# Seven block products in place of eight in two feed-forward networks, with the hidden activations sent through DRAM

## The chip, the cores and the metric

The kernel runs on one core of one Trainium2 chip. Its time is the device time of one execution in microseconds, the median of several runs. Engines are named as in the profile: PE is TensorE (matmuls), PEld its weight loads, DVE is VectorE, ACT is ScalarE, POOL is GpSimd and SP is SyncE, which here issues every DMA.

## The reference

Two transformer layers, one after the other, on 1024 tokens of 1024 features in fp32. What the change touches are their two feed-forward networks, each with 2816 hidden features (22 tiles of 128):

```python
# layer 1
x = layer_norm(DEEPNORM_ALPHA * x + einsum('bse,ed->bsd', mix, w_out), ln1_g, ln1_b)
gate, up = (x @ w_gu)[..., :FFN_HIDDEN], (x @ w_gu)[..., FFN_HIDDEN:]
ffn = (silu(gate) * up) @ w_down
x = layer_norm(DEEPNORM_ALPHA * x + ffn, ln2_g, ln2_b)
...
# layer 2
x = x + gate_m * rmsnorm(mix, g_mix_post)
h = rmsnorm(x, g_ffn_pre) * (1.0 + scale_f) + shift_f
f = (silu(h @ w_gate) * (h @ w_up)) @ w_down
x = x + gate_f * rmsnorm(f, g_ffn_post)
```

The vectors `scale_f`, `shift_f` and four more come from one product of a condition vector with `w_cond`, which the kernel works out beside the first network.

## The kernel before

Every product of fp32 matrices is made of three matmuls: an operand is split into `hi` (a cast, on ACT, line 80) and `lo` (the rest, a subtraction, mostly on DVE, line 84), and hi·hi, hi·lo and lo·hi are added in PSUM. So each 128 x 128 block of weights times 512 tokens costs three matmuls of 128x512.

The activations stand feature-major, hi and lo, in tiles for each half of the tokens (`Act`). `Act.put` turns one token block of 128 by eight transposes on PE (line 766), casts on ACT (line 777) and subtracts on DVE (line 778). Blocks 0 to 3 are the first half, blocks 4 to 7 the second; in the trace the tiles are x10 and x11 for the first network and x30 and x31 for the second (with h or l for the part).

`ffn` runs over the 22 hidden tiles. For a tile and a half of the tokens `gate_up` makes 48 matmuls (eight feature tiles, gate and up, three each), then silu on ACT (line 835), the product (line 836) and the split of the result on DVE and ACT. The result stays in SBUF. After every two tiles `down` multiplies them with two row tiles of the down weights (lines 863 to 865), block after block of tokens, and DVE adds 128x512 pieces into the accumulators `acc` (line 720 in the first network, 1319 in the second). The last four tiles (three in the second network) end each token block with its residual and norm (`after`). The first two tiles take the first half of the tokens first: their 96 matmuls need nothing of the second half.

Layer 1's output projection and norm stand ahead of the first network (lines 693 to 695, 717, 720, 784 to 797), layer 2's ahead of the second (line 1179 to 1197). Beside the first network `cond(j)` works out the vectors of layer 2: six chunks of eight 512 KB loads and eight DVE steps (line 949), one after every third tile.

A scheduler orders the rows of each engine as the code is written; what stands under `soon()` is moved ahead. All engines run their rows in order. The loads of weights and those of layer 2's residuals go through one queue, SP.

Of the kernel before, what the change touches and what calls it, by code (L numbers as in the profile page):

```python
# [38 lines left out]
def two_blocks(ctx: ExitStack, tc: tile.TileContext, a):  # L39
# [55 lines left out]
    def mm3(out, lh, ll, rh, rl, start, stop):  # L95
        T.matmul(out, lh, rh, start=start, stop=False)  # L96
        T.matmul(out, lh, rl, start=False, stop=False)  # L97
        T.matmul(out, ll, rh, start=False, stop=stop)  # L98

    def rsqrt(v, n):  # L100
        """v: [P, n] -> 1/sqrt(v); v is overwritten"""
# [18 lines left out]
    # =====================================================================  # L120
    # block 1: input projection, indexer selection, attention, gMLP
    # =====================================================================
# [59 lines left out]
    # DRAM scratch  # L182
# [5 lines left out]
    # indexer keys (hi, lo, hi, lo over the partitions), indexer weights, values of C  # L188
# [17 lines left out]
    # the first token blocks follow the arrival of x  # L206
# [38 lines left out]
    class TopkSet:  # L245
# [39 lines left out]
        def settle(self):  # L285
            """a sign sum counts a tie by half: the result is the threshold or the number before it"""
# [17 lines left out]
        def mask(self):  # L304
            """scores -> additive mask with the distances; ties at the threshold go to the lowest keys"""
# [13 lines left out]
    def load_qk(pl, bufs, src, s):  # L319
        """[hi; hi], [lo; lo] of the queries and [hi; lo] of the keys of one head over 128 partitions"""  # L320
# [23 lines left out]
    def expo(qk, i, bias, slope):  # L344
        """exp(logits - max) and its sum; the products come divided by slope"""
# [30 lines left out]
    # pieces of the projections, to be put between the steps of other work  # L376
# [11 lines left out]
    def qk_pieces(u):  # L388
        """queries (scaled) and keys of a head of B or of two of C, hi and lo, to DRAM"""
# [123 lines left out]
    class Paced:  # L513
        """runs a generator at so many steps a turn"""
# [16 lines left out]
    # 1 - lam_init goes into the gain; neglam = -lam  # L531
# [14 lines left out]
    class LaneB:  # L546
        """a head of B after the other: weights() and then mix() of one token block after the other"""
# [52 lines left out]
    class LaneC:  # L600
        """the heads of C in pairs"""
# [71 lines left out]
    def turned(tb, c0):  # L673
        """columns c0 .. c0 + 512 of token block tb of the mixers' outputs, feature-major, hi and lo"""
# [11 lines left out]
    def out_block(wo, mt, tb, put):  # L686
        """half of the contraction of the output projection for token block tb"""
# [124 lines left out]
    def norm1(tb):  # L812
        layer_norm(acc[tb], g1, b1, G, V)
# [617 lines left out]
```

## Time and profile before

| what | value |
| --- | --- |
| median of three runs | 2656.75 us (2655.37 to 2658.04) |
| span of the profiled execution | 2659.7 us |
| PE busy | 2500.7 us, 94% |
| DVE busy | 1494.9 us, 56% |
| ACT busy | 916.3 us, 34% |
| POOL busy | 355.8 us, 13% |
| DMA | 262.91 MB, 99 GB/s on average |

The profiled execution's span lies 2.95 us above the median of the runs. The network of layer 1 runs from about 660 to 1425 us, that of layer 2 from about 1890 to the end. Matmuls overlap one another, so a PE at 100.00 us in 100 us says that it never stopped, not that no matmul could be packed closer.

### The profile page before, as it was taken

How to read it: one execution, taken by the hardware profiler on the slowest of the kernel's cores; microseconds unless marked ns; L12 is line 12 of the kernel's file. 1: busy time of each engine (PE TensorE's matmuls, PEld its weight loads, DVE VectorE, ACT ScalarE, POOL GpSimd, SP SyncE). 2: the span in 40 equal slices, each digit the busy share in tenths (PEclk: the TensorE clock that was granted, in tenths of full speed). 3: DMA queues.
4: the chain of work that ended last, by engine and by line, in shares of the span. 5: the costliest groups of instructions: out<-in, count | busy, mean ns of one | idle time of the engine just before them, and what ended most of it. 6: DMA issues, size and time to landing. Idle time of an engine off the chain costs nothing. (4 is left out here: it accounts for less than half of the span.)

```text
span 2659.7 us, 32099 instructions
## 1 busy us (share of the span) xinstructions
PE 2500.7 (94%) x12232; PEld 2068.2 (78%) x12232; DVE 1494.9 (56%) x2974; ACT 916.3 (34%) x1603; POOL 355.8 (13%) x250
## 2 busy tenths in 40 slices
PE   8889897899999999999999988898899999999997
PEld 8878776787778878878887777786688888888885
DVE  3889869648544444444367366768923333333337
ACT  4558774343211111111145235455731111111111
POOL 2220233112000000000020044327200000000002
PEclk9999998999999999999999999899999999999999
DMA  5154455422433232332223534643511111111112
GB/s 180 56 150 116 114 160 169 112 78 65 135 95 104 97 101 86 100 115 87 64 88 123 158 91 136 187 130 101 173 50 46 48 48 48 48 48 48 48 48 103
DMA packets 129333, 262.91 MB, mean 99 GB/s; under 512 B 17302, under 2 KB 63382, under 8 KB 129180
## 3 DMA queue, kind: packets, MB, share of 16 engines
q1 hardware_dynamic: 129180, 260.87, 31.7%
q8 instruction: 96, 1.57, 0.2%
q14 instruction: 57, 0.47, 0.1%
HBM read 206.27 MB, written 54.55 MB: 98 GB/s over the span
## 5 line engine op out<-in xcount | busy, mean ns | idle before, releaser
L80 ACT CAST wh<-raw 128x1024 fp32r<-128x1024 f32 x132 | 138.3, 1049 | 467.7 <-PE plg L97 381.7
L1319 DVE TENSOR_TENSOR acc<-acc,pmm 128x512 f32<-128x512 f32 x160 | 109.6, 686 | 233.9 <-PE pmm L865 232.9
L863 PE MATMUL pmm<-wdh,hh 128*128 128x512 f32 x576 | 227.9, 396 | 6.9 <-DVE acc L1319 3.8
L84 DVE TENSOR_TENSOR wl<-raw,wh 128x1024 fp32r<-128x1024 f32 x107 | 130.8, 1223 | 176.9 <-ACT wh L80 144.4
L865 PE MATMUL pmm<-wdh,hl 128*128 128x512 f32 x576 | 226.4, 393 | 0.0
L864 PE MATMUL pmm<-wdl,hh 128*128 128x512 f32 x576 | 226.4, 393 | 0.0
L720 DVE TENSOR_TENSOR acc<-acc,pmm 128x512 f32<-128x512 f32 x160 | 109.0, 684 | 147.1 <-PE pmm L865 140.8
L835 ACT ACTIVATE silu<-plg 128x512 f32<-128x512 f32 x88 | 52.2, 594 | 350.4 <-PE plg L98 350.3
L338 PE MATMUL plg<-qk,qk 128*128 128x384 f32 (+4 forms) x480 | 125.2, 376 | 21.1 <-DVE mn L351 6.7
L96 PE MATMUL plg<-x10h,wh 128*128 128x512 f32 x352 | 139.6, 397 | 4.9 <-ACT wh L80 4.9
L96 PE MATMUL plg<-x30h,wh 128*128 128x512 f32 x352 | 140.3, 400 | 1.4 <-ACT x30h L777 1.4
L97 PE MATMUL plg<-x30l,wh 128*128 128x512 f32 x352 | 140.4, 399 | 0.7 <-DVE x30l L778 0.7
L98 PE MATMUL plg<-x30h,wl 128*128 128x512 f32 x352 | 140.0, 398 | 0.0
L98 PE MATMUL plg<-x10h,wl 128*128 128x512 f32 x352 | 139.4, 396 | 0.1
L97 PE MATMUL plg<-x31l,wh 128*128 128x512 f32 x352 | 139.5, 396 | 0.0
L98 PE MATMUL plg<-x31h,wl 128*128 128x512 f32 x352 | 139.5, 396 | 0.0
L96 PE MATMUL plg<-x11h,wh 128*128 128x512 f32 x352 | 139.4, 396 | 0.0
L97 PE MATMUL plg<-x10l,wh 128*128 128x512 f32 x352 | 139.4, 396 | 0.0
L96 PE MATMUL plg<-x31h,wh 128*128 128x512 f32 x352 | 139.2, 396 | 0.0
L98 PE MATMUL plg<-x11h,wl 128*128 128x512 f32 x352 | 139.0, 395 | 0.0
L97 PE MATMUL plg<-x11l,wh 128*128 128x512 f32 x352 | 139.0, 395 | 0.0
L863 PEld LDWEIGHTS pmm<-wdh,hh 128*128 128x128 f32 x576 | 108.6, 189 | 36.5 <-DVE acc L1319 8.2
(351 smaller groups left out, 6306.4 us busy)
## 6 DMA issues: line engine op xcount, KB each, us to landing
raw<-in_wgu_dram SPq DMA_DIRECT2D x50, 512.0 KB, 3.6
raw_c<-in_w_cond_dram SPq DMA_DIRECT2D x48, 512.0 KB, 3.9
raw<-in_w_down_dram SPq DMA_DIRECT2D x44, 512.0 KB, 3.5
qk<-qkd SPq DMA_DIRECT2D x72, 256.0 KB, 6.5
qk<-qk2d SPq DMA_DIRECT2D x48, 256.0 KB, 4.8
raw<-in_wg_dram SPq DMA_DIRECT2D x22, 512.0 KB, 3.5
raw<-in_wu2f_dram SPq DMA_DIRECT2D x22, 512.0 KB, 4.0
raw<-in_wqk_dram SPq DMA_DIRECT2D x20, 512.0 KB, 3.7
```

The costliest lines, as they stand in the source:

```text
L80: A.copy(hi, src)
L84: eng.tensor_tensor(lo, src, hi.bitcast(F32), op=OP.subtract)
L96: T.matmul(out, lh, rh, start=start, stop=False)
L97: T.matmul(out, lh, rl, start=False, stop=False)
L98: T.matmul(out, ll, rh, start=False, stop=stop)
L338: T.matmul(pl[:, c, :n], q[:, isl], k2[:, c * n:(c + 1) * n], start=(j == 0), stop=last)
L720: V.tensor_tensor(acc[tb][:, dsl], acc[tb][:, dsl], o, op=OP.add)
L835: A.activation(s, pg[:, 0, :], AF.Silu)
L863: T.matmul(o, hh[:, ts], wh[:, dsl], start=(j == 0), stop=False)
L864: T.matmul(o, hh[:, ts], wl[:, dsl], start=False, stop=False)
L865: T.matmul(o, hl[:, ts], wh[:, dsl], start=False, stop=(j == n - 1))
L1319: V.tensor_tensor(acc2[tb][:, dsl], acc2[tb][:, dsl], o, op=OP.add)
```

## The change

Both networks are computed with Strassen's scheme (in Winograd's form): a matrix product of halves is made of seven block products and sums of blocks, where the plain way takes eight. All names below are those of the changed kernel.

For gate and up, `SAct` keeps the activations as quarters B11, B21, B22 (features by tokens) and the sums T1, T2, T3, T4, each in hi and lo parts. `put` of blocks 0 to 3 writes B11 and B21; `put` of blocks 4 to 7 writes B22, T3, T1 and T2, which need both halves of the tokens; `finish` makes T4 when all blocks are there. `Matrix` holds two hidden tiles of gate or of up, makes the weights' sums S1 to S4 on DVE, splits each operand, and runs seven products of 12 matmuls; `after` adds the products up. Eleven pairs of tiles take 11 x 2 x 7 x 12 = 1848 matmuls. The result goes to DRAM (`h_d`, line 992).

`down` then loads hidden tiles and down weights back (line 1065), 18 tiles in groups of 2 x (1, 2, 2, 2, 2), again as seven products each, with their sums and splits on DVE and POOL; the seven accumulators are combined in the last group. `down_last` does the last four tiles the plain way, and ends each token block. Layer 1's normed output goes to DRAM too (`x1_d`) and is added in `residual1`. `cond` runs after the pairs 1 to 6 of the first network.

The core of the diff:

```diff
+        def put(self, x, tb, affine=None):
...
+            t1, t2, t3 = self.temp(), self.temp(), self.temp()
+            V.tensor_tensor(t1, b12, b11[0], op=OP.subtract)
+            A.copy(t3, b22)
+            G.tensor_tensor(t1, t1, b11[1], op=OP.subtract)
+            V.tensor_tensor(t3, t3, b12, op=OP.subtract)
+            self.part("B22", ts, b22, V)
+            V.tensor_tensor(t2, b22, t1, op=OP.subtract)
+            self.part("T3", ts, t3, V)
+            self.part("T1", ts, t1, G)
+            self.part("T2", ts, t2, V)
+
+        def finish(self):
+            (bh, bl), (th, tl) = ([t.bitcast(F32) for t in self(n)] for n in ("B21", "T2"))
+            for c in range(4):
+                ts = slice(c * P, (c + 1) * P)
+                t = self.temp()
+                G.tensor_tensor(t, bh[:, :, ts], th[:, :, ts], op=OP.subtract)
+                G.tensor_tensor(t, t, bl[:, :, ts], op=OP.add)
+                G.tensor_tensor(t, t, tl[:, :, ts], op=OP.subtract)
+                self.part("T4", ts, t, G if c % 2 else V)
...
+        LEFT = {1: "A11", 6: "S2", 2: "A12", 7: "S3", 5: "S1", 4: "A22", 3: "S4"}
+        RIGHT = {1: "B11", 6: "T2", 2: "B21", 7: "T3", 5: "T1", 4: "T4", 3: "B22"}
...
+        def product(self, p):
...
+                A.copy(wh, x)
+                (G if p in (2, 4) else V).tensor_tensor(wl, x, wh.bitcast(F32), op=OP.subtract)
+            xh, xl = self.act(self.RIGHT[p])
+            first = p in (1, 6, 7, 5)
+            for k in range(4):
+                mm3(o, wh[:, k, :], wl[:, k, :], xh[:, k, :], xl[:, k, :], first and k == 0, k == 3, not first)
+            with soon():
+                self.after(p, o)
...
+            DMA.dma_start(h_d[self.f + i][:, l * 512:(l + 1) * 512], s)
...
+            if p == 0:
+                order = ((0, 1), (1, 1), (0, 2), (1, 2), *((m, q) for m in range(2) for q in (6, 7, 5, 4, 3)))
+            else:
+                order = tuple((m, q) for m in range(2) for q in (1, 6, 2, 7, 5, 4, 3))
...
+        def combine(p, c0, n):
+
+            x = {q: acc_of(q, c0, n) for q in range(1, 8)}
+            if p == 2:
+                G.tensor_tensor(x[2], x[2], x[1], op=OP.add)
+            elif p == 6:
+                G.tensor_tensor(x[6], x[6], x[1], op=OP.add)
+            elif p == 7:
+                G.tensor_tensor(x[7], x[7], x[6], op=OP.add)
+            elif p == 4:
+                G.tensor_tensor(x[4], x[7], x[4], op=OP.subtract)
+            elif p == 5:
+                V.tensor_tensor(x[6], x[6], x[5], op=OP.add)
+                G.tensor_tensor(x[7], x[7], x[5], op=OP.add)
+            elif p == 3:
+                V.tensor_tensor(x[3], x[6], x[3], op=OP.add)
...
+        for g, np_ in enumerate(sizes):
+            hr = [load2([h_d[f + np_ * i + j][:, :] for j in range(np_)], "hr") for i in range(2)]
+            wr = [load2([wd(f + np_ * i + j) for j in range(np_)], "wr") for i in range(2)]
...
+                        "S1": ("A21", "A22", OP.add, V), "S2": ("S1", "A11", OP.subtract, V),
+                        "S3": ("A11", "A21", OP.subtract, G), "S4": ("A12", "S2", OP.subtract, G),
+                        "T1": ("B12", "B11", OP.subtract, G), "T2": ("B22", "T1", OP.subtract, V),
+                        "T3": ("B22", "B12", OP.subtract, G), "T4": ("T2", "B21", OP.subtract, V)}[n]
...
+                    split(*hl, x, lo_eng="pool" if p in (1, 2, 4) else "dve")
+                    split(*wl, z, lo_eng="pool" if p in (1, 3) else "dve")
...
+                        if g == 0:
+                            A.copy(x, o)
+                        else:
+                            V.tensor_tensor(x, x, o, op=OP.add)
+                    if g == len(sizes) - 1:
+                        combine(p, c0, n)
...
+                split(*t, r, lo_eng="pool" if to is hs else "dve")
...
-    def extra1(ft):
-        if ft % 3 == 1 and ft // 3 < 6:
-            cond(ft // 3)
+    def extra1(p):
+        if 1 <= p <= 6:
+            cond(p - 1)
...
+    SIZES, NLAST = (1, 2, 2, 2, 2), 4
+    gate_up(x1, lambda f: a["wgu"][f], lambda f: a["wgu"][NFT + f], 5, 8, extra1)
...
+    y1 = down(dp, lambda f: a["w_down"][f], SIZES)
...
+    down_last(tp, lambda f: a["w_down"][f], NLAST, y1, residual1, after1, lambda: put_half(0))
```

Where rows stand on the engines, at three places.

On PE at the start of the second network the kernel before has the first tile's matmuls on the first half of the tokens (x30) right behind the output projection and a transposed block (L766); further blocks are transposed between them, and x31 comes after 96 of them and more:

```order
L695 MATMUL pmm<-woh_15234,mixl 128x512
L766 MATMUL ptr<-ident,acc 128x128 x8
L96 MATMUL plg<-x30h,wh 128x512 x2
L97 MATMUL plg<-x30l,wh 128x512
L98 MATMUL plg<-x30h,wl 128x512
```

In the changed kernel the same place reads as follows; x3B21 belongs to the first half of the tokens and is the last of the 48 matmuls of products 1 and 2, x3T2 is the operand of product 6:

```order
L98 MATMUL pmm<-x3B21l,wst 128x512
L99 MATMUL pmm<-x3B21h,wst 128x512
L815 MATMUL ptr<-ident,acc 128x128 x24
L97 MATMUL ptr<-x3T2h,wst 128x512
L98 MATMUL ptr<-x3T2l,wst 128x512
L99 MATMUL ptr<-x3T2h,wst 128x512
```

The transposes of the last three token blocks moved behind all matmuls on the first half, and the next matmul reads a sum to which every block of the second half contributes.

On DVE at the start of the first network, in the changed kernel, these rows follow the last token block (x1T2l is the last part of T2, x1T4l the parts of T4 whose input POOL makes, L922 the sums of weights and L943 the lo part of a weight operand, the first being that of product 6):

```order
L805 TENSOR_TENSOR x1T2l<-tt,x1T2h 128x4x128
L805 TENSOR_TENSOR x1T4l<-tt,x1T4h 128x4x128
L922 TENSOR_TENSOR tt<-rw 128x512
L805 TENSOR_TENSOR x1T4l<-tt,x1T4h 128x4x128
L922 TENSOR_TENSOR tt<-tt,rw 128x512
L922 TENSOR_TENSOR tt<-rw 128x512
L943 TENSOR_TENSOR wst<-tt,wst 128x512
```

The operand S2 of product 6 (the second L922 row) stands behind both parts of T4, which product 4 reads later on.

On SP between gate/up and down of the second network (the first network has the same rows), and on POOL at the end of the last down group (L84 lo parts, L1051 to L1058 combinations, `last` the hidden tiles of the plain end):

```order
L992 DMA h_d_6888<-p_19636 128x512
L992 DMA h_d_6887<-u_19658 128x512
L1065 DMA hr<-h_d_6867 128x1024
L1065 DMA hr<-h_d_6868 128x1024
L1065 DMA wr<-in_w_down_dram 128x1024 x2
```

```order
L84 TENSOR_TENSOR ws<-wr,ws 128x1024
L1055 TENSOR_TENSOR acc<-acc 128x512 x2
L1055 TENSOR_TENSOR acc<-acc 128x2x512
L1058 TENSOR_TENSOR acc<-acc,dacc_10151 128x512 x2
L1058 TENSOR_TENSOR acc<-acc,dacc_10151 128x2x512
L84 TENSOR_TENSOR last<-raw,last 128x1024 x4
```

In both, what the next stage needs first stands behind the last row of the stage before; before the change neither of these rows existed, since the hidden tiles never left SBUF.

## Rows read from the trace of the kernel before

**Rows 1.** The page: span, instructions, busy time of each engine.

```profile
span 2659.7 us, 32099 instructions
PE 2500.7 (94%) x12232; PEld 2068.2 (78%) x12232; DVE 1494.9 (56%) x2974; ACT 916.3 (34%) x1603; POOL 355.8 (13%) x250
```

**Rows 2.** Windows inside each network: length, busy us by engine (instructions), PEclk, DMA share, GB/s.

```profile
1000.00:1100.00 100.00, 100.00 (x432) 80.84 (x431) 46.77 (x57) 17.31 (x22) 0.00 (x0) 1.00 0.31 95
2200.00:2300.00 100.00, 100.00 (x431) 80.86 (x430) 33.25 (x43) 15.29 (x20) 0.00 (x0) 1.00 0.16 53
```

**Rows 3.** Waits of PE from 690 to 1400 us: total, times, longest.

```profile
PE pmm L863 <- DVE acc L720: 1.6, 3, 0.8
```

**Rows 4.** Windows at the networks' starts and ends, columns as in rows 2.

```profile
640.00:660.00 20.00, 19.62 (x92) 15.43 (x93) 19.36 (x46) 9.54 (x12) 4.80 (x2) 1.00 0.28 86
660.00:680.00 20.00, 13.65 (x61) 10.46 (x60) 19.42 (x30) 9.85 (x13) 5.55 (x2) 0.83 0.51 160
...
1400.00:1420.00 20.00, 16.17 (x75) 12.95 (x74) 18.62 (x61) 9.92 (x20) 4.80 (x2) 0.90 0.14 54
1860.00:1880.00 20.00, 17.48 (x81) 13.70 (x80) 19.76 (x57) 14.22 (x26) 7.68 (x4) 1.00 0.72 236
1880.00:1900.00 20.00, 13.98 (x57) 10.27 (x56) 19.86 (x59) 14.89 (x26) 3.09 (x1) 0.83 0.72 240
1900.00:1920.00 20.00, 20.00 (x96) 16.32 (x95) 17.52 (x60) 15.80 (x30) 4.80 (x2) 1.00 0.34 122
...
2609.00:2646.00 37.00, 31.67 (x125) 23.86 (x124) 33.46 (x75) 8.06 (x14) 15.55 (x7) 0.95 0.36 127
```

**Rows 5.** Groups by line and shape, 700 to 1450 us: busy, mean ns.

```profile
L720 DVE TENSOR_TENSOR acc<-acc,pmm 128x512 f32<-128x512 f32 x144 | 98.1, 684 | 141.3 <-PE pmm L865 140.8
L84 DVE TENSOR_TENSOR wl<-raw,wh 128x1024 fp32r<-128x1024 f32 x51 | 62.3, 1222 | 54.7 <-ACT wh L80 54.4
L949 DVE SCALAR_TENSOR_TENSOR mod<-raw_c,sc,mod 128x1024 f32<-128x1024 f32 x35 | 45.0, 1285 | 53.8 <-DMA raw_c<-in_w_cond_dram 53.8
L796 POOL TENSOR_TENSOR acc<-acc,g 128x1024 f32<-128x1024 f32 x6 | 14.5, 2422 | 709.7 <-ACT acc L795 703.7 <-PE pmm L865 6.0
```

**Rows 6.** Timeline of DVE, three neighbours: start, length.

```profile
1886.33 1.21 DVE L84 TENSOR_TENSOR wl<-raw,wh 128x1024 fp32r<-128x1024 f32 x1
1887.46 0.68 DVE L1179 TENSOR_TENSOR acc<-acc,pmm 128x512 f32<-128x512 f32 x1
1888.06 1.22 DVE L84 TENSOR_TENSOR wl<-raw,wh 128x1024 fp32r<-128x1024 f32 x1
```

**Rows 7.** Timeline: last put of layer 1's norm, PE around it.

```profile
674.03 0.79 PE L96 MATMUL plg<-x10h,wh 128*128 128x512 f32 x1 [4.92 <-ACT wh L80]
676.78 0.80 PE L96 MATMUL plg<-x11h,wh 128*128 128x512 f32 x1
...
678.76 1.27 DVE L778 TENSOR_TENSOR x11l<-ptr,x11h 128x512 fp32r<-128x512 f32 x2
```

**Rows 8.** Timeline: POOL and DVE side by side, 1799 to 1849 us.

```profile
1799.98 9.13 POOL L84 TENSOR_TENSOR wol<-raw,woh 128x1024 fp32r<-128x1024 f32 x3 [2.85 <-ACT woh L80]
1807.48 2.71 DVE L1227 TENSOR_TENSOR sab<-sab 128x1023 f32<-128x1023 f32 x1
...
1830.82 4.51 POOL L1174 TENSOR_TENSOR mixrow<-mixrow 128x512 f32<-128x512 f32 x2 [2.13 <-DMA mixrow<-mixT_d]
1834.67 0.68 DVE L1179 TENSOR_TENSOR acc<-acc,pmm 128x512 f32<-128x512 f32 x1
1848.68 2.56 POOL L1174 TENSOR_TENSOR mixrow<-mixrow 128x512 f32<-128x512 f32 x2 [1.97 <-DMA mixrow<-mixT_d]
```

**Rows 9.** Timeline: PE at the second network's start; last put.

```profile
1892.13 1.22 PE L96 MATMUL plg<-x30h,wh 128*128 128x512 f32 x2 [1.45 <-ACT x30h L777]
...
1934.43 0.69 DVE L778 TENSOR_TENSOR x31l<-ptr,x31h 128x512 fp32r<-128x512 f32 x1
```

**Rows 10.** DMA issues: KB each, median us from issue to landing.

```profile
raw<-in_w_down_dram SPq DMA_DIRECT2D x44, 512.0 KB, 3.5
```

More of the change, by code (lines that the diff above doesn't have):

```diff
@@ L93, in load_split, with mm3 @@
         return h, l
[L95 to L98, printed above, removed]
+    def mm3(out, lh, ll, rh, rl, start, stop, more=False):
+        T.matmul(out, lh, rh, start=start, stop=False, skip_group_check=more)
+        T.matmul(out, lh, rl, start=False, stop=False, skip_group_check=more)
+        T.matmul(out, ll, rh, start=False, stop=stop, skip_group_check=more)
     def rsqrt(v, n):
@@ L737, in two_blocks @@
     p1_done.close()
-    actp, act_done = pool("actp")
+    x1p, x1_done = pool("x1p")
     class Act:
@@ L809, in two_blocks @@
     b1 = row(slot("w", [P, D], F32, "ln1b"), a["ln1_b"])
-    x1 = Act(actp, "x1")
+    x1 = SAct(x1p, "x1")
+    x1_d = dr.tile([S, D], F32, name="x1_d")
     def norm1(tb):
         layer_norm(acc[tb], g1, b1, G, V)
+        DMA.dma_start(x1_d[tb * P:(tb + 1) * P, :], acc[tb])
     out_proj(wo, lambda tb: turned(tb, 512), add1, norm1, lambda tb: x1.put(acc[tb], tb), 2)
+    x1.finish()
     wo_done.close()
@@ new lines, in two_blocks, with out @@
+    class Gate(Matrix):
+        def out(self, i, l, t, o):
+            if t is None:
+                t = self.post("s11")
+                A.activation(t, o, AF.Silu)
+            else:
+                A.activation(t, t, AF.Silu)
+            self.p[i, l] = t
+    class Up(Matrix):
+        def out(self, i, l, t, o):
+            s = self.gate.p[i, l]
+            if t is None:
+                V.tensor_tensor(s, s, o, op=OP.mult)
+            else:
+                G.tensor_tensor(s, s, t, op=OP.mult)
+            DMA.dma_start(h_d[self.f + i][:, l * 512:(l + 1) * 512], s)
@@ new lines, in gate_up, with load, post @@
+    def gate_up(act, wg, wu, nraw, npost, extra=None):
+        gp, gp_done = pool("gp")
+        n_raw = [0]
+        def load(src):
+            n_raw[0] += 1
+            shape = [P, KT, P]
+            if nraw < 4 and n_raw[0] % 5 >= nraw:
+                r = slot("raw", shape, F32, "raw")
+            else:
+                r = gp.tile(shape, F32, tag="rw", bufs=nraw, name="rw")
+            DMA.dma_start(r, src)
+            return r
+        def post(nm):
+            return gp.tile([P, 512], F32, tag="post", bufs=npost, name=nm)
+        for p in range(NFT // 2):
+            f = 2 * p
+            if p == 0:
+                order = ((0, 1), (1, 1), (0, 2), (1, 2), *((m, q) for m in range(2) for q in (6, 7, 5, 4, 3)))
+            else:
+                order = tuple((m, q) for m in range(2) for q in (1, 6, 2, 7, 5, 4, 3))
+            ms = {}
+            for m, q in order:
+                if m not in ms:
+                    w = (wg, wu)[m]
+                    ms[m] = (Gate, Up)[m]([load(w(f)), load(w(f + 1))], act, post)
+                    if m == 1:
+                        ms[1].gate, ms[1].f = ms[0], f
+                ms[m].product(q)
+            if extra is not None:
+                extra(p)
+        gp_done.close()
@@ new lines, in down_last @@
+    def down_last(tp, wd, nlast, y, start, after, between=None):
+        hs, ws = [], []
+        for n in range(nlast):
+            f = NFT - nlast + n
+            for src, to in ((h_d[f][:, :], hs), (wd(f), ws)):
+                r = slot("raw", [P, S], F32, "raw")
+                DMA.dma_start(r, src)
+                if to is ws and n < 3:
+                    t = [slot("w", [P, S], F32R, "last") for _ in range(2)]
+                else:
+                    t = [tp.tile([P, S], F32R, tag="last", bufs=10, name="last") for _ in range(2)]
+                split(*t, r, lo_eng="pool" if to is hs else "dve")
+                to.append(t)
+        for tb in range(NB):
+            if start is not None:
+                start(y, tb)
+            if tb == NB // 2 and between is not None:
+                between()
+            ts = slice(tb * P, (tb + 1) * P)
+            for dh in range(2):
+                dsl = slice(dh * 512, (dh + 1) * 512)
+                o = ps_mm(512)
+                for j in range(nlast):
+                    T.matmul(o, hs[j][0][:, ts], ws[j][0][:, dsl], start=(j == 0), stop=False)
+                    T.matmul(o, hs[j][0][:, ts], ws[j][1][:, dsl], start=False, stop=False)
+                    T.matmul(o, hs[j][1][:, ts], ws[j][0][:, dsl], start=False, stop=(j == nlast - 1))
+                V.tensor_tensor(y[tb][:, dsl], y[tb][:, dsl], o, op=OP.add)
+            after(y, tb)
@@ L1300, in two_blocks @@
     x3p, x3_done = pool("x3p", "right")
-    x3 = Act(x3p, "x3")
+    x3 = SAct(x3p, "x3")
     n = 0
```

294 lines of the change are left out of this document (173 added, 121 removed).

## The prediction

> **What bounds the kernel now.** I read the page first. PE is busy 94% of a span of 2659.7 us, DVE 56%, POOL 13% [rows 1]. Then the windows inside the two networks: PE 100.00 us of 100, 432 matmuls, granted clock 1.00, while DVE has half its time free and POOL does nothing [rows 2]. The waits of PE confirm it: from 690 to 1400 us it waited 1.6 us in all [rows 3]. So inside a network every matmul taken away is time gained, and one costs 100/432 = 0.2315 us. The windows at the starts and ends look different [rows 4]: from 640 to 680 and from 1860 to 1900 us DVE is full (19.4 to 19.9 of 20 us) and PE is the one that waits, 13.65 and 13.98 of 20 us with the clock down to 0.83. At the very end, 2609 to 2646 us, DVE has 33.46 of 37 us. These stretches belong to DVE; what is added there is paid for.
>
> **What the change takes away.** Before: 22 tiles x 2 halves x 48 = 2112 matmuls for gate/up and 22 x 8 x 2 x 3 = 1056 for down, 3168 a network. After: 1848 for gate/up; down has seven products of 84 for a pair of tiles in each half and nine such pairs, of which the group sizes make 756 matmuls in all, and the last four tiles take 4 x 48 = 192; together 2796. Difference 372 a network, 744 in all: **-172.2 us**, the full gain if PE never waited. The rest of the sum is where it does.
>
> Durations for that: DVE takes a new row every 1.13 us for 128x1024 and every 0.60 us for 128x512 [rows 6], against recorded means of 1222 and 684 ns [rows 5]. POOL takes 2.42 us for 128x1024 [rows 5] and 2.56/2 = 1.28 us for 128x512 with two inputs [rows 8].
>
> **Start of the first network.** DVE ends its last put at 678.76 + 1.27 = 680 us [rows 7], and has been full for 40 us. Counting the rows of its order from the first add of the output projection to this place: 18 more rows of 128x512 in the puts and T4 (10.8 us), 13 more of cond (1.2 us each, 15 us), less 5 us of weight splits that move away: +21 us. S2 of product 6 stands behind T4, whose parts need nine to twelve POOL rows of 1.28 us after the last T2: +12 us. Then S2, its cast and its lo part, 3 us. Product 6 starts near 716 us. Until then PE has only the 48 matmuls of products 1 and 2 (11 us). Before, it flows from 677 us [rows 7] and had done 56. 716 - 677 + 8 x 0.23 = **+41**. Lower bound: if those cond rows and POOL rows slip beside idle DVE time, only the chain of 12 us is left.
>
> **Start of the second network.** Before, the last put ends at 1935 us, but PE has worked on x30 since 1892 us [rows 9], full from 1900 on [rows 4]; by 1942 us it has done some 207 matmuls. After, DVE's rows stay nearly the same in sum (18 more of 0.60 us, ten weight splits of 1.13 us fewer), so T4, S2 and product 6 come at about 1942 us, and PE has been able to do 48. (207 - 48) x 0.2315 = **+37**; lower bound again the POOL chain, 12.
>
> **cond.** One chunk in each of six pairs of 168 matmuls (38.9 us), where it had 100 us. DVE has 29 own rows of 128x512 in a pair (8 sums of weights, 10 lo parts, 11 on the products: 17.4 us), about 5 us of waiting beside POOL's seven rows and 13 us of cond (8 to 10 rows of 1285 ns [rows 5]): 36 of 38.9. I give it **+4**, between nothing and, where the loads bind, 48 (rival C).
>
> **From gate/up to down.** The first loads of down stand on SP behind the last write of h. So after PE's last product there follow in a chain: POOL's product of 128x512 (1.7 us at its price beside DVE), the write (about 3 us), two hidden tiles and a row tile of weights, of which the first lands after 3.5 us [rows 10] and each further 512 KB takes 524288 B / 240 GB/s [rows 4] = 2.2 us, that is 7.9 us, a cast and a lo part on POOL (2 us): 15 us. POOL's row for the weights of product 3 in this small first group stands behind sums that need the second group's loads, 3 us more. **+36** for both networks; bounds 16 and 60.
>
> **Steady groups of down.** DVE has 34 rows a group, 14 of 0.60 and 20 of 1.13 us: 31.0 us, beside 168 matmuls, 38.9 us. POOL, idle before, has nine rows of 128x1024. What happens when both are at work is in [rows 8]: three POOL subtractions took 9.13 us, 3.04 each instead of 2.42, and a DVE row with two SBUF inputs 2.71 us instead of 1.2; the DVE row at 1834.67 us, which reads PSUM, took its usual 0.68 beside a busy POOL. So I add about 1.3 us of waiting for each POOL row to DVE: 31.0 + 11.7 = 42.7, 3.8 over PE. Three groups, two networks: **+23**; bounds nothing (all in gaps) and rival B.
>
> **Last group.** POOL has its nine rows (21.8 us), the combinations, five of 2 x 1.28 + 2.42 us (24.9 us), and then the lo parts of the four last hidden tiles (9.7 us), in this order, 56 us without sharing and some 63 with it. The first block of `down_last` needs all four. PE has 38.9 us of matmuls for that time, with a lead of 3 us: **+42** for both; bounds 20 and 60.
>
> **Ends.** Layer 1: a block now has 24 matmuls, 5.6 us, and on DVE a residual (1.2 us), two adds, the norm's rows and modulation, about 7.7 us; over eight blocks 17 us, where before the gate/up of the second half of the tokens covered the first half's norm; with 2 us of the first put **+19**. Layer 2's end had been DVE's [rows 4]; it has about the same rows and PE a little less: **-4**.
>
> **Clock.** After a wait of some us the granted clock is 0.83 over 20 us [rows 4], about 3.4 us lost. Three to four more of these stretches than before: **+12**.
>
> **Sum.** -172 + 41 + 37 + 4 + 36 + 23 + 42 + 19 - 4 + 12 = +38. Against the profiled execution's 2659.7 us that is 2697.7; that execution lies 2.95 us above the median of the runs, so **2695 us**, slower by 1.4%. A difference under 0.2%, 5.3 us, is about what a measurement of this kernel can't tell from none.
>
> **A rule that speaks against the change.** The Trainium skill, Perfetto Trace Analysis, section Optimizing Scalar/DVE Operations, says that GpSimd and DVE share a read port, so that handing work from one to the other might not help. In [rows 8] the trace agrees for rows with two SBUF inputs and not for the one that reads PSUM. Taken without that exception the rule is rival B; with it the sum stays as it is.
>
> **Rivals.** *A, the starts cost only their chain.* Then the scheduler's order hides cond and the sums in DVE's gaps, and product 6 starts 12 us after the last put in both networks: 24 in place of 78, 2641 us, faster. For it: PE's own waits at 660 to 680 us are only some 6 us [rows 4], and from 1900 to 1920 us DVE has 2.5 us free. Against it: DVE is full before. It decides from the point where both starts together cost under 40 us.
>
> *B, DVE and POOL exclude each other altogether in down.* Then a group takes 31.0 + 9 x 2.42 = 52.8 us in place of 42.7: 10 more in six steady groups, 60 us, or 2755 us. For it: POOL's 3.04 us and DVE's 2.71 us [rows 8]. Against it: the PSUM row that ran beside POOL, and 14 + 7 of 34 rows of a group read PSUM.
>
> *C, loads starve the first network.* cond's eight loads of 512 KB and four of gate/up in 38.9 us are 162 GB/s beside 1 MB of h writes, 190 in all, through one queue in which a load waits for a free buffer and holds up those behind it; 8 us a pair for six pairs is 48, 2743 us. For it: before, the loads ran at 95 GB/s [rows 2], half of that. Against it: 240 GB/s were moved at 1880 to 1900 us [rows 4].
>
> **Chances.** Forecast 0.50 (its own range 2650 to 2735, with a twelfth of it below 2651 us), A 0.27, B 0.15, C 0.08. Faster by over 0.2%: A and the forecast's lower edge, 0.31; within 0.2%: 0.07; slower: 0.62. The range for 8 in 10 takes in most of A (with down's waiting gone as well: 2641 - 23 - 18 = 2600) and B with a little of C (2755 + 15): 2600 to 2770.
>
> **What would show it.** In the changed profile: about 11490 PE records in place of 12232 [rows 1]. PE still at 0.2315 us a matmul inside gate/up of the second network. PE idle between the 48 first matmuls and the first one on T2, ended by a DVE or ACT row that waits for POOL; 20 to 30 us of it in each start. A gap of about 15 us at each first `hr` load, ended by a DMA or a cast. DVE over 90% busy in steady groups, with rows of two SBUF inputs near 2 us. POOL busy without a break through the last group. Wrong if the gaps at the starts are under 10 us each (A), if steady groups take over 48 us (B), or if PE waits for `wst` behind DMA in the first network's pairs (C).

## The result and the profile after

The changed kernel takes 2729.99 us (median of four, 2728.08 to 2732.15) against 2657.32 us before: 1.0273 times as long, 95% interval 1.0259 to 1.0288. It is slower, as forecast and inside the range; the likeliest value, 2695 us, was 35 us too low.

First the page of the changed kernel, with the rows that answer to [rows 1]:

```profile
span 2728.3 us, 32599 instructions
PE 2393.6 (88%) x11488; PEld 1953.5 (72%) x11488; DVE 1931.6 (71%) x3364; ACT 1112.7 (41%) x1951; POOL 963.4 (35%) x576
```

744 matmuls are gone, exactly as counted, and PE is busy for 107 us less. The span still grew by 68.6 us, so PE's idle time grew by some 175 us. PE's busy time fell by less than 172 us in part because more matmuls ran at a low granted clock: 395 of those with 512 columns begin 0.30 to 0.47 us after the one ahead of them, 240 in the trace of before, where 0.234 us is the spacing at a granted clock of 1.00. Over that spacing they cost 59 and 32 us, an estimate of 27 us for the change. Where the idle time lies is seen in windows of 50 us (columns as in [rows 2]): both starts, a stretch of the first network's gate/up, the step to down, the end of down, and, for comparison, gate/up of the second network.

```profile
650.00:700.00 50.00, 27.82 (x96) 20.42 (x97) 48.52 (x73) 15.60 (x25) 21.76 (x11) 0.74 0.66 234
700.00:750.00 50.00, 26.75 (x104) 20.45 (x103) 30.81 (x40) 14.38 (x25) 27.94 (x20) 0.72 0.14 46
...
850.00:900.00 50.00, 44.84 (x185) 35.60 (x184) 36.95 (x44) 12.99 (x23) 12.58 (x7) 0.93 0.57 182
...
1250.00:1300.00 50.00, 49.13 (x209) 38.61 (x207) 50.00 (x44) 16.93 (x17) 33.76 (x13) 1.00 0.32 113
...
1350.00:1400.00 50.00, 36.72 (x141) 27.98 (x139) 42.70 (x33) 12.19 (x12) 49.87 (x21) 0.84 0.17 59
...
1950.00:2000.00 50.00, 23.92 (x95) 16.99 (x93) 44.05 (x111) 38.18 (x76) 19.56 (x13) 0.71 0.22 82
2000.00:2050.00 50.00, 29.53 (x116) 23.21 (x117) 32.01 (x39) 14.38 (x25) 27.49 (x20) 0.75 0.17 58
...
2250.00:2300.00 50.00, 50.00 (x215) 40.20 (x214) 28.72 (x38) 14.72 (x25) 13.46 (x10) 1.00 0.24 79
```

In the second network's gate/up PE never stops. At the starts it works for about half of 100 us, at a granted clock of 0.71 to 0.75. In the first 50 us of each start DVE is nearly full (48.52 and 44.05 us); in the second 50 us no engine is, and the time goes into a chain that runs over POOL, ACT and DVE in turn, shown below. From 1250 to 1300 us DVE is busy for all 50 us and PE for 49.13.

PE's timeline names the gaps (start, length; in brackets the idle time ahead and what ended it): the first matmul on T2 in each network, the first of down, the first network's wait in the plain end.

```profile
723.12 0.80 PE L97 MATMUL ptr<-x1T2h,wst 128*128 128x512 f32 x1 [22.30 <-ACT wst L942]
1188.52 0.79 PE L1107 MATMUL pmm<-ws,hs 128*128 128x512 f32 x1 [11.15 <-ACT ws L80]
1395.50 0.79 PE L1146 MATMUL pmm<-last 128*128 128x512 f32 x1 [6.43 <-POOL last L84]
2020.07 0.79 PE L97 MATMUL ptr<-x3T2h,wst 128*128 128x512 f32 x1 [23.95 <-ACT wst L942]
```

The forecast had product 6 of the first network at 716 us; it came at 723.12. Behind the 22 us stands the chain that it named. In the timeline of POOL, DVE and ACT, POOL works through T4 (L848 to L850), DVE waits for it with its row T4l, and the row L922 at 720.78, which is S2, comes only then; its cast releases PE.

```profile
711.93 4.60 POOL L849 TENSOR_TENSOR tt<-tt,x1B21l 128x512 f32<-128x512 f32 x3
712.66 1.09 DVE L805 TENSOR_TENSOR x1T4l<-tt,x1T4h 128x512 fp32r<-128x512 f32 x1 [6.68 <-ACT x1T4h L804]
713.78 1.63 DVE L922 TENSOR_TENSOR tt<-rw 128x512 f32<-128x512 f32 x1
716.50 3.70 POOL L850 TENSOR_TENSOR tt<-tt,x1T2l 128x512 f32<-128x512 f32 x3
719.66 1.09 DVE L805 TENSOR_TENSOR x1T4l<-tt,x1T4h 128x512 fp32r<-128x512 f32 x1 [4.25 <-ACT x1T4h L804]
720.78 1.63 DVE L922 TENSOR_TENSOR tt<-tt,rw 128x512 f32<-128x512 f32 x1
722.45 0.62 ACT L942 CAST wst<-tt 128x512 fp32r<-128x512 f32 x1 [1.60 <-DVE tt L922]
```

Cut at landmarks of PE (last matmul of the output projection, first on T2, last of gate/up, first of down, last of the plain end, first of the next part), each stage's length less 0.2315 us for each of its matmuls, beside the same of the kernel before, gives this table, in us:

| term | forecast | measured |
| --- | --- | --- |
| matmuls removed | -172 | -172 |
| start, first and second network | +41, +37 | +44, +41 |
| rest of gate/up, first and second network | +4, 0 | +32, +11 |
| step to down with its first group, both | +36 | +43 |
| three steady groups, both | +23 | +8 |
| last group, plain end and what follows, first network | +42/2 + 19 = +40 | +54 |
| the same, second network | +42/2 - 4 = +17 | +15 |
| clock, named apart | +12 | in the stages |
| the part between the networks | 0 | +2 |
| lost inside the networks before the change | 0 | -9 |
| sum | +38 | +69 |

From the end of layer 2's output projection to the end of the span it was 774.5 us before and is 777.3 us now: the second network is a draw (forecast +3). The first lost 64 us (forecast +35); 4.6 of them, booked with its start, lie ahead of the first landmark, as layer 1's output projection itself ends later (659.2 against 654.7 us). Nearly all of the 31 us that the forecast lacked lie in the first network, and 28 of them in one term, the one with cond.

The waits of DVE from 750 to 1180 us (total, times, longest) have one line that the second network hasn't:

```profile
DVE mod L1170 <- DMA raw_c<-in_w_cond_dram: 34.8, 24, 3.6
```

PE's waits in the same stretch, of which the second network (2050 to 2447 us) has 0.9 us for L968 and none for L963:

```profile
PE plg L97 <- DVE p L968: 12.3, 6, 5.2
PE plg L97 <- DVE u L963: 2.9, 3, 2.0
```

DVE is busy for 268 of these 430 us, so over the whole stretch it isn't short of time. It stands for 34.8 us in front of cond's loads, in order, and the sums of the products (L963 to L973) queue behind; PE waits for the banks that they read. The wait for these loads is not new: before the change it was 53.8 us in 35 rows [rows 5], and PE lost 1.6 us [rows 3]. From the first matmul on T2 the pairs 1 to 6 of the first network take 40.7, 45.6, 47.4, 41.6, 47.3 and 40.7 us, the pairs 7 to 9, which have no cond, 39.2 each.

### The profile page after: what moved, and what is told of

The parts are those of the page before. It is cut to its first block, busy times and chain, and to the rows that moved or that the text cites. A ratio compares the mean times of both kernels' runs of the same rounds, so it can differ in the third digit from the quotient of the medians.

```text
span 2728.3 us, 32599 instructions
## 1 busy us (share of the span) xinstructions
PE 2393.6 (88%) x11488; PEld 1953.5 (72%) x11488; DVE 1931.6 (71%) x3364; ACT 1112.7 (41%) x1951; POOL 963.4 (35%) x576
## 5 line engine op out<-in xcount | busy, mean ns | idle before, releaser
L942 ACT CAST wst<-tt 128x512 fp32r<-128x512 f32 x176 | 109.1, 621 | 309.3 <-PE plg L99 260.9
L943 POOL TENSOR_TENSOR wst<-rw,wst 128x512 fp32r<-128x512 f32 x61 | 87.1, 1429 | 345.5 <-ACT wst L942 187.8
L84 POOL TENSOR_TENSOR wl<-raw,wh 128x1024 fp32r<-128x1024 f32 (+2 forms) x28 | 68.7, 2460 | 248.6 <-ACT wh L80 220.1
L943 DVE TENSOR_TENSOR wst<-tt,wst 128x512 fp32r<-128x512 f32 x176 | 125.2, 712 | 15.6 <-ACT wst L942 14.7
L280 ACT ACTIVATE junk_a<-xi,cand 128x1024 bf16<-128x1024 f32 (+1 forms) x124 | 108.8, 878 | 14.9 <-DVE cand L269 6.7
L1458 DVE TENSOR_TENSOR_SCAN sab<-sab 128x640 f32<-128x640 f32 (+7 forms) x64 | 101.1, 1585 | 19.0 <-ACT sab L1456 18.4
L339 PEld LDWEIGHTS plg<-qk,qk 128*128 128x128 f32 x480 | 80.6, 195 | 31.1 <-DVE mn L352 11.6
L1107 PE MATMUL plg<-ws,hs 128*128 128x512 f32 x252 | 101.9, 404 | 1.1 <-DVE acc L1115 1.0
L1108 PE MATMUL plg<-ws,hs 128*128 128x512 f32 x252 | 101.0, 401 | 0.0
L1109 PE MATMUL plg<-ws,hs 128*128 128x512 f32 x252 | 100.8, 400 | 0.0
L164 PE MATMUL pmm<-wh,xh 128*128 128x256 f32 (+1 forms) x320 | 93.0, 291 | 3.1 <-DVE stgl L401 1.8
L943 POOL TENSOR_TENSOR wst<-raw,wst 128x512 fp32r<-128x512 f32 x27 | 39.4, 1461 | 150.4 <-issue 85.8
L166 PE MATMUL pmm<-wh,xl 128*128 128x256 f32 (+1 forms) x320 | 91.9, 287 | 0.0
L165 PE MATMUL pmm<-wl,xh 128*128 128x256 f32 (+1 forms) x320 | 91.8, 287 | 0.0
L84 POOL TENSOR_TENSOR hs<-hr,hs 128x1024 fp32r<-128x1024 f32 (+1 forms) x30 | 82.2, 2740 | 13.4 <-ACT hs L80 13.4
```

Of the source, the lines that this page charges most:

```text
L84: eng.tensor_tensor(lo, src, hi.bitcast(F32), op=OP.subtract)
L164: T.matmul(o, at(0, k, tb * P, P), h[:, j, :], start=(k == 0), stop=False)
L165: T.matmul(o, at(0, k, tb * P, P), l[:, j, :], start=False, stop=False)
L166: T.matmul(o, at(1, k, tb * P, P), h[:, j, :], start=False, stop=(k == KT - 1))
L280: A.activation(junk_a[:, :L], xi[self.blks[i]], AF.Sign, bias=c, accum_out=self.cnt[:, i:i + 1])
L339: T.matmul(pl[:, c, :n], q[:, isl], k2[:, c * n:(c + 1) * n], start=(j == 0), stop=last)
```

## The experiments

All times are medians, each beside runs of the kernel before on the same chip. The kernel before took 2657.3 to 2660.7 us there, so a difference of some 3 us between runs is not clear. The traces move too where nothing was edited: from the first matmul on T2 to the end of gate/up the first network takes 454.3 us in the changed kernel and 460.5 and 459.6 us in two runs below (no GpSimd in down's groups, the last lo parts on DVE), whose rows up to there are the same in the same order; why isn't known. So small differences are read in the stages that an edit touches, cut at the landmarks of the table. The order is that in which they ran.

**T4 later.** The call that makes T4 moves behind the issue of products 6 and 7 of the first pair.

```diff
-    x1.finish()
...
+                if p == 0 and (m, q) == (0, 5):
+                    act.finish()
                 ms[m].product(q)
```

> The parts of T4 are made after products 6 and 7 of the first pair are issued, so S2 and its split stand right behind T2 on VectorE. Theory (T4's GpSimd chain holds up S2 and so product 6): the first matmul on T2 moves from 723.1 to about 709 us in the first network and by about as much in the second; since product 4 comes 8.3 us after product 6 and still needs T4, some of it is given back: 10 to 24 us in all, 2706 to 2720 us. Rival (VectorE's own rows set the start, T4 only fills a wait that is there anyway): under 4 us, 2726 us or more.

2724.45 us, 5.5 less: outside the expected 2706 to 2720, though the place was right. In its PE timeline the first matmul on T2 stands at 709.40 us, 13.7 earlier, as foretold:

```profile
709.40 0.79 PE L97 MATMUL ptr<-x1T2h,wst 128*128 128x512 f32 x1 [6.78 <-ACT wst L941]
720.05 0.47 PE L97 MATMUL plg<-x1T1h,wst 128*128 128x512 f32 x1 [0.88 <-DVE u L962]
730.63 0.79 PE L97 MATMUL plg<-x1T4h,wst 128*128 128x512 f32 x1 [7.55 <-ACT x1T4h L804]
```

and 7.55 us are lost again in front of product 4, a wait that was 0.55 us. The first pair ends 1.1 us earlier than in the changed kernel. T4's chain did hold up product 6, and it holds up whatever reads T4 as well.

**One load for cond.** Each chunk loads one tile of w_cond and uses it eight times, which leaves out seven eighths of the condition's product.

```diff
-            r = slot("raw", [P, D], F32, "raw_c")
-            DMA.dma_start(r, a["w_cond_2"][k * P:(k + 1) * P, j * D:(j + 1) * D])
+            if k == 0:
+                r = slot("raw", [P, D], F32, "raw_c")
+                DMA.dma_start(r, a["w_cond_2"][k * P:(k + 1) * P, j * D:(j + 1) * D])
```

> Each chunk of cond loads one 512 KB tile and uses it eight times: VectorE's rows are the same, seven of eight loads are left out, and with them the values of the condition's vectors. Theory (VectorE, in order, waits for these loads, and the product sums behind it keep TensorE waiting): pairs 1 to 6 of the first network fall from 40.7 to 47.4 us to about 40.3 us each, 18 to 22 us less, 2708 to 2712 us. Rival (the eight VectorE rows of a chunk are themselves too many beside a pair): no change, 2730 us.

2707.35 us, 22.6 less, just past the theory's 2708. The pairs 1 to 6 take 40.1 to 40.7 us each. Of DVE's wait for these loads only that for the first of each chunk is left (750 to 1160 us; it was 5.1 us):

```profile
DVE mod L1169 <- DMA raw_c<-in_w_cond_dram: 4.8, 3, 2.6
```

DVE's rows are the same as before the edit, so it wasn't their number. The edit takes away the wait and most of the traffic together; it can't tell them apart.

**cond in every other pair.**

```diff
-        if 1 <= p <= 6:
-            cond(p - 1)
+        if p in (1, 3, 5, 7, 9, 10):
+            cond((1, 3, 5, 7, 9, 10).index(p))
```

> cond's chunks run after pairs 1, 3, 5, 7, 9 and 10 in place of 1 to 6. Theory of crowding (loads of neighbouring chunks and of the pair's weights stand in each other's way): 10 to 21 us less, 2709 to 2720 us. Rival (each chunk costs its own latency of loads, wherever it stands): within 5 us of 2730.

2718.65 us, 11.3 less, in the theory's range: half of what the loads cost. DVE still waits for them, for 40.9 us from 750 to 1165 us, but it hurts PE less, as the pairs now take 40.2 to 44.9 us. So crowding makes about half of the loss. What makes the other half no run shows.

**The second network alone.** Layer 1 has the network of the kernel before.

> Layer 1 keeps the network of the kernel before; only layer 2's is changed. From the landmarks of the two traces (end of layer 2's output projection to the end of the span: 774.5 before, 777.3 after) the second network alone costs 3 us and the first 64: 2660 us, between 2655 and 2665. If part of the first network's 64 us belonged to what both share, 2675 or more.

2664.58 us, 1.0025 of before (1.0014 to 1.0035), at the upper end of what was expected. The draw of the second network is confirmed to within a few us (780.2 us from the end of the output projection, against 777.3 and, before, 774.5), and so, by difference (2729.99 less 2664.58), are the first network's 64 us.

**Product 4 last.** As the first run, and the first pair runs 6, 7, 5, 3 of gate and of up, then both products 4; T4 is asked for at product 7 of up.

```diff
-                order = ((0, 1), (1, 1), (0, 2), (1, 2), *((m, q) for m in range(2) for q in (6, 7, 5, 4, 3)))
+                order = ((0, 1), (1, 1), (0, 2), (1, 2), *((m, q) for m in range(2) for q in (6, 7, 5, 3)), (0, 4), (1, 4))
```

> As e1, and in the first pair product 4, the only one that reads T4, comes last, after products 6, 7, 5 and 3 of gate and of up (96 matmuls, 22 us later than product 6). e1 brought product 6 forward by 14 us and lost 7.5 us again in waiting for T4. Theory (only T4's GpSimd chain is between): the first network's first pair ends about 14 us sooner than in the changed kernel, the second's about 15: 2700 to 2705 us. Rival (behind T4 the weights' sums or bank reuse hold PE anyway): 2718 or more.

2721.18 us, 8.8 less, in the rival's range. The first network's first pair ends 9.0 us sooner, not 14, and 2.5 of these are left at the end of gate/up, as pairs 1 to 6 take longer (41.9, 48.6, 46.9, 41.8, 49.7 and 40.7 us); the second network is 4.6 us shorter. PE no longer waits for T4, but for the weights' sum of up's product 7, which DVE makes behind T4l:

```profile
706.14 0.79 PE L97 MATMUL ptr<-x1T2h,wst 128*128 128x512 f32 x1 [6.77 <-ACT wst L941]
720.33 0.50 PE L97 MATMUL plg<-x1B22h,wst 128*128 128x512 f32 x1 [0.78 <-DVE u L964]
729.09 0.80 PE L97 MATMUL plg<-x1T3h,wst 128*128 128x512 f32 x1 [5.69 <-ACT wst L941]
```

**cond held back from the start.** The condition vector passes through a row that reads T4 times zero, so DVE's 15 rows of cond can't stand among the last puts.

```diff
+        if p == 1:
+            V.scalar_tensor_tensor(sc, x1("T4")[0].bitcast(F32)[:, 0, S // 2 - KT:S // 2], 0.0, sc,
+                                   op0=OP.mult, op1=OP.add)
         if 1 <= p <= 6:
```

> The changed kernel, but cond's VectorE rows can't begin before T4 is there (the condition vector is passed through a row that reads T4 times zero), so the 15 rows that stood among the last puts of the first network come after product 6's operands. My prediction counted them with 15 us of the start. By it the first matmul on T2 moves from 723.1 to about 708 us; the rows then stand beside gate/up, which has room for part of them: 2715 to 2722 us. Rival (the puts wait for the output projection and the norm anyway, cond fills gaps): T2 moves by under 4 us, 2727 to 2735 us.

2717.60 us, 12.4 less, in the expected range. The first matmul on T2 comes at 703.27 us, 20 us earlier, more than the 15 counted; 7 us are given back by the end of gate/up, 4.4 in the first pair (36.1 us in place of 31.7) and 2.9 in pairs 1 to 6 (pair 2 takes 48.4 us).

```profile
703.27 0.79 PE L97 MATMUL ptr<-x1T2h,wst 128*128 128x512 f32 x1 [22.01 <-ACT wst L942]
```

The wait of 22 us itself stays: most of it is T4's, as it fell to 6.78 us in the run with T4 later, and it comes after the puts whenever these end.

**No GpSimd in down's groups.** All sums and lo parts go to DVE (`lo_eng="dve"` in both splits, V in place of G in the table of sums); the combinations stay.

> In down's groups all sums and lo parts are on VectorE, none on GpSimd (the combinations in the last group stay there). VectorE then has 20 to 43 rows a group, 31.0 + 9 x 1.13 = 41.2 us, without anything beside it. If the two engines exclude each other for rows with two SBUF inputs, GpSimd's share was worth little: a steady group goes from 40.2 to 41 to 42 us, and the last group loses its wait for GpSimd: 2715 to 2735 us in all. If GpSimd's nine rows ran free beside VectorE, each moved row costs its 1.13 us: VectorE had 31 and now 41 us, a group 41 too, but the trace would then show VectorE under 85% busy in the changed kernel, where it shows 100%.

2726.17 us, 3.8 less. Nine rows of 1.2 us in each steady group went from POOL to DVE, and the group stayed where it was: 39.2 to 41.1 us, against 40.0 to 40.3. The first group fell from 30.5 to 21.1 us in the first network and from 28.9 to 22.1 in the second: there PE had waited for a lo part that POOL makes (the changed kernel's timeline):

```profile
1214.99 0.79 PE L1108 MATMUL pmm<-ws,hs 128*128 128x512 f32 x1 [4.08 <-POOL ws L84]
```

From the end of gate/up on, the two networks are 8.0 and 4.9 us shorter than in the changed kernel (296.1 and 275.8 us). That the total fell by 3.8 only goes with the gate/up of the first network, unedited and 6.3 us longer in this trace. The same window of steady groups in the changed kernel and in this run:

```profile
1250.00:1350.00 100.00, 98.45 (x418) 77.67 (x417) 100.00 (x88) 34.12 (x34) 62.52 (x23) 1.00 0.20 74
1250.00:1350.00 100.00, 97.15 (x414) 77.36 (x413) 100.00 (x105) 33.93 (x34) 0.88 (x1) 1.00 0.18 63
```

DVE is full with POOL at work and without. The groups of DVE by form from 1255 to 1345 us say why (mean ns last before the idle time). In the changed kernel:

```profile
L84 DVE TENSOR_TENSOR hs<-st,hs 128x1024 fp32r<-128x1024 f32 x9 | 14.5, 1611 | 0.0
L1115 DVE TENSOR_TENSOR acc<-acc,plg 128x1024 f32<-128x1024 f32 x9 | 10.9, 1206 | 0.0
L84 DVE TENSOR_TENSOR ws<-wr,ws 128x1024 fp32r<-128x1024 f32 x3 | 9.5, 3178 | 0.0
L1089 DVE TENSOR_TENSOR st<-wr,st 128x1024 f32<-128x1024 f32 x2 | 6.1, 3042 | 0.0
```

and with POOL out of it:

```profile
L84 DVE TENSOR_TENSOR hs<-st,hs 128x1024 fp32r<-128x1024 f32 x9 | 10.9, 1206 | 0.0
L1115 DVE TENSOR_TENSOR acc<-acc,plg 128x1024 f32<-128x1024 f32 x9 | 10.8, 1201 | 0.0
L84 DVE TENSOR_TENSOR ws<-wr,ws 128x1024 fp32r<-128x1024 f32 x7 | 8.4, 1206 | 0.0
```

A row with two SBUF inputs takes 1206 ns alone and, by the means of these groups, 1611 to 3178 ns beside POOL; a row that reads PSUM (plg) takes 1206 and 1201.

**The last hidden tiles' lo parts on DVE.**

```diff
-                split(*t, r, lo_eng="pool" if to is hs else "dve")
+                split(*t, r, lo_eng="dve")
```

> The lo parts of the last four hidden tiles are made on VectorE in place of GpSimd, where they stand behind 25 us of combinations. PE waited 14.0 us for them in both networks together. Theory (the order on GpSimd is what the plain end waits for): 8 to 14 us less, 2716 to 2722 us. Rival (VectorE, 100% busy in this group, is as late): within 4 us of 2730.

2735.78 us, 5.8 more, which neither line had. The extra time isn't at the edit: the first network's gate/up, ahead of it, ends 8.5 us later than in the changed kernel, and from there on the networks take 302.2 and 279.6 us, 1.9 and 1.1 less. That is the rival's "within 4 us". In the first network PE still waits 5.37 us there, now for DVE, and the next token blocks wait for DVE's sums too. The order on POOL alone isn't the cause.

```profile
1401.28 0.79 PE L1146 MATMUL pmm<-last 128*128 128x512 f32 x1 [5.37 <-DVE last L84]
1405.79 0.73 PE L1144 MATMUL pmm<-last 128*128 128x512 f32 x2 [1.06 <-ACT last L80]
1409.63 1.22 PE L1144 MATMUL pmm<-last 128*128 128x512 f32 x2 [0.95 <-ACT last L80]
1414.85 0.79 PE L1144 MATMUL pmm<-last 128*128 128x512 f32 x1 [1.83 <-DVE acc L1147]
```

**Down the plain way, both networks, then the second alone, then with product 4 last.** Hidden tiles come from DRAM, nine groups of two tiles, no sums of blocks; the last four tiles as in the change, with all lo parts on DVE.

```diff
-    y2 = down(dp2, lambda f: a["w_down_2"][f], SIZES)
+    y2 = plain_down(dp2, lambda f: a["w_down_2"][f], NFT - NLAST)
```

> The changed kernel with down the plain way in both networks: hidden tiles and down weights come back from DRAM in nine groups of two tiles, 96 matmuls each, added by VectorE alone; gate/up stay seven products. Theory (down's seven products save 25 us of matmuls a network and cost more than that, at their start 11.6 + 9.5 to 11, in steady groups 4, in the last group 8 and at the plain end part of 17 to 20): 15 to 25 us less a network, 2680 to 2700 us. Rival (the trip of the hidden tiles through DRAM is what costs, which stays): 2730 plus 50 of matmuls less little, 2750 us or more.

> Layer 1's network as before the change, layer 2's with seven products in gate/up and the plain down of the run above. By the same theory 2664.6 - 20 = 2640 to 2650 us, faster than before the change; by the rival 2675 or more.

> As the run above, and the first pair's products in the order of the run with product 4 last. That order took 4.7 us off the second network of the changed kernel: 3 to 5 us less than the run above, 2636 to 2647 us.

2724.04, 2671.00 and 2663.52 us. The first is 6 us under the changed kernel, not 30 to 50; the second 6.4 us over the run with the second network alone, not 15 to 25 under it. No total came as either line had it, but the stages of the first run do take sides. From the end of gate/up on, in us (changed kernel, then plain down):

| stage | first network | second network |
| --- | --- | --- |
| step to down | 11.2, 0.8 | 11.6, -0.2 |
| down's groups (108 matmuls more, 25 us) | 199.3, 216.8 | 196.7, 221.9 |
| plain end | 63.9, 48.3 | 62.0, 53.4 |
| to the next part, or the end | 29.8, 18.4 | 10.5, 10.5 |
| sum | 304.1, 284.3 | 280.7, 285.7 |

In the first network the theory's 15 to 25 us came, 19.9; what the seven products cost there is the step, 10 us, and 27 us in the plain end and behind it. In the second they are 5.0 us better than the plain way (3.5 between the two runs with the second network alone, 284.2 and 287.7 us). The gain of the first run's total is smaller in part because its unedited gate/up of the first network took 6.3 us more. PE's waits in the second of the runs from 1950 us on say what the plain way kept (the first line is the start's wait for product 6):

```profile
PE ptr L97 <- ACT wst L1043: 24.0, 1, 24.0
PE pmm L1240 <- DVE acc L1247: 9.0, 9, 1.2
PE pmm L1274 <- ACT last L80: 3.9, 3, 2.9
PE pmm L1241 <- DVE op L84: 3.7, 1, 3.7
PE pmm L1240 <- ACT op L80: 3.5, 1, 3.5
```

PE waits nine times for a bank (L1247), up to 1.2 us, where the kernel before had gate/up between two groups. The first group of two tiles takes 35.0 us in this run for 96 matmuls (22.2 us), so a down that stands by itself pays a start of its own in the plain form too. The theory that the seven products are what costs down holds for the first network and fails for the second. The order with product 4 last gave 7.5 us here.

**The second network alone, with product 4 last and no GpSimd in the first group.**

> Only layer 2's network in seven products, with product 4 last in the first pair and no GpSimd rows in down's first group. From the runs so far: 2664.6 for the second network alone, less 4.7 (product 4 last) and less 3 to 8 (first group 28.9 to 22.1 us where GpSimd was left out, part of it lost again): 2652 to 2657 us, 1 to 7 us under the kernel before. Rival: each removed wait comes back at the next place, as in the runs on T4: 2659 us or more.

2652.15 us, 0.9971 of before (0.9959 to 0.9984), as expected: 0.3% under the kernel before, which is little, but the interval leaves out 1. From the end of the output projection to the end of the span it takes 768.9 us, against 780.2 in the run with the second network alone and 774.5 before. So 5.6 of the 9.4 us between this trace and that of before are the second network's; the rest lies in layers of the same code. T2's first matmul came 16 us earlier and 6 of them reached down. Of the first group's 6.7 us almost nothing was left: the second group took 45.9 us where it had 40.0.

## Why the prediction was right

**The sign and the main terms** held. The removal is 744 matmuls of 0.2315 us; the starts, the step to down and the end cost more than that together. The two starts (44 and 41 us against 41 and 37) were worked out from DVE's full windows in [rows 4] and the counted rows, and the runs bear out both halves of the first: cond's rows among the puts (20 us of T2's time, 15 forecast) and T4's chain (14 us, 12 forecast). Rival A, starts of 12 us, is ruled out by the two starts' 85 us, where it needed under 40; even with S2 freed of T4 or cond held back, each alone, product 6 came no earlier than 703 us, 23 us after the last put of the kernel before [rows 7]. The two edits together were not run.

**Where the forecast was lucky.** The second start's +37 is two errors that nearly cancel. By 1942 us the trace of before has 175 matmuls of the network, not some 207, as 38 transposes stood among them: 7 us too much. And product 6 came 68.6 us after the output projection, which is 1954 us on the clock of before and not 1942: 12 us too little. The step to down (+36 for 43) also came out of parts that missed: 15 us to the first matmul of down measured 11, and 3 us in the first group measured 11 and 9.5, of which 4.1 in each are a wait for POOL. The result lies 35 us from the likeliest value and inside a range that is 170 us wide.

**The term that was too small** is cond, "+4, between nothing and, where the loads bind, 48". It was reckoned as DVE's busy time in a pair, 36 of 38.9 us, and taken near the lower bound. What it left out is DVE's wait for the loads, which stood in the forecast's own [rows 5]: 53.8 us of idle time before 35 rows, ended by the loads. In the changed kernel it is 34.8 us before 24 rows, and now PE's banks hang on the sums behind it. The run with one load puts this at 22.6 us. Why the loads come late isn't settled. SP's own waits ahead of them, from 750 to 1180 us, end with an earlier load of cond or with the row that reads one:

```profile
SPq L1166 <- DMA raw_c<-in_w_cond_dram: 51.2, 22, 4.3
SPq L1166 <- DVE mod L1170: 31.2, 23, 1.9
```

These loads share three buffers with others, so too few buffers is as likely a cause as the writes of h ahead of them on SP; the kernel before had no such writes and DVE waited as well. Neither was varied. Rival C named such loads at 48, but its sign, PE waiting for `wst` behind a DMA, isn't among PE's waits, and 182 GB/s in the window shown, against 240 in [rows 4], do not look like a limit of bandwidth.

**The rest of gate/up** adds about 10 us in each network that no term had: the first pair 31.0 us against 27.8, the last 41.3, and the pairs between 39.36 against 168 x 0.2315 = 38.9 in the second network. About 5 of the 10 us are no loss at all: 0.2315 us is a mean over gate/up and down, and gate/up's matmuls cost 0.234 us before the change too (last section). Of the last pair I know the size only.

**The clock**, +12 by itself, is inside the measured terms; the estimate from the spacing of matmuls, above, is 27 us.

**The term that was too large** is the steady groups, +23 against +8. The price of 1.3 us for each POOL row was taken for all nine; a group came to 40.2 us in place of 42.7, and DVE's rows that read PSUM went on at 1206 ns beside POOL. Rival B, 52.8 us a group, is ruled out by the same rows. The Trainium skill, Perfetto Trace Analysis, section Optimizing Scalar/DVE Operations, has the rule that an offload between GpSimd and DVE might not help, for the port they share. Here the run without POOL agrees for the steady groups: nine rows moved back cost nothing that can be seen in a group (39.2 to 41.1 us against 40.0 to 40.3).

**Ends.** The first network's was 14 us longer than forecast. After its last matmul 30 us pass to the first one of the next part, where there had been 5. In the trace PE's transposes wait there for DVE's rows of x20 (9.04, 6.89 and 3.50 us). The run with the last lo parts on DVE leaves the plain end and these 30 us as they were together (93.4 us against 93.7); the run with plain down in both cuts them to 66.7. So this loss, too, comes from the seven products' last group and not from those lo parts; which of its rows does it no run shows.

## What to carry to other kernels

Here fewer matmuls did not pay, because the work that makes their operands did not fit beside them: count the sums, splits and accumulations for each matmul removed, and look at the places where the first operand needs the last input. On an engine that works in order, a row that waits for a late load costs what queues behind it, however idle the engine is on average; so for small side work beside a faster main loop add its waits to its busy time, also those that cost nothing before. A difference of a few us in a total should be looked for in the stage that was edited before it is believed: in two runs here the stage moved the other way than the total, or three times as far. And a wait that is taken out should be followed to the next one in the same chain before it is booked as a gain: here 14 us brought 5.5.

## What was not expected of the hardware

Beside POOL a DVE row of 128x1024 with two SBUF inputs took 1.6 to 3.2 us in place of 1.21, and one with an input in PSUM its usual 1.21; nine POOL rows a steady group bought DVE no time. In the first group of down, where PE waited for POOL, moving them to DVE did help (30.5 to 21.1 us).

A price per matmul that is read over a whole network is a mean of two. In the trace of before, with PE never idle, 62 matmuls of gate/up take 14.52 us, 0.234 each, and the 12 of down behind them 2.77 us, 0.231 each:

```profile
2199.76 0.40 PE L97 MATMUL plg<-x30l,wh 128*128 128x512 f32 x1
2214.28 0.40 PE L863 MATMUL pmm<-wdh,hh 128*128 128x512 f32 x1
2217.05 0.39 PE L96 MATMUL plg<-x30h,wh 128*128 128x512 f32 x1
```

Inside gate/up of the seven products it is 39.36/168 = 0.2343 us, the same price. Why the matmuls of down stand closer stays open.
